# A hybrid decoder layer in float32: the head by token tile, another order of units and transfers, small products in fewer slots

## The chip, the core and the metric

The kernel runs on one core of a Trainium2 chip. The core has TensorE (PE; its weight loads are shown apart as PEld), VectorE (DVE), ScalarE (ACT) and GpSimd (POOL), each with an instruction stream of its own that it works off in order, and SyncE (SP), which here only issues DMA transfers. The engines wait for one another through semaphores. The metric is the device time of one execution in microseconds (us), lower is better. The kernel before takes 151.75 us, the median of 3 runs (151.47 to 152.13).

## What is computed

256 tokens of width 1024 go through a layer norm, one input projection, four causal mixers side by side, an output projection and a last layer norm. Cut to what matters:

```python
h    = layernorm(x, emb_ln_g, emb_ln_b)                 # x: 256 x 1024, float32
proj = h @ w_in                                         # 15 column groups of 256 (and 4 columns for dt)
y_ssd  = ssd(z, conv4(xbc), dt)                         # Mamba-2: causal convolution, silu, chunks of 128
y_hgrn = rms(chunk_scan(q, f = sigmoid(h_f), i)) * silu(h_g)
y_ret  = groupnorm(retention(q, k, v)) * silu(r_g)
y_moba = softmax(q k^T + alibi) v * silu(m_g)           # block-sparse attention, here one own block
y   = concat(y_ssd, y_hgrn, y_ret, y_moba) @ w_out      # 1024 x 1024
out = layernorm(2 ** 0.25 * h + y, ln_g, ln_b)          # 256 x 1024
```

## The kernel before, in words

**Products.** The two projections are done with exact halves of float32: an operand is cast to fp32r (`hi`), and the rest is `lo = x - hi`. A product is then hi·hi + hi·lo + lo·hi. A unit is one column group of 256. It has two halves (128 channels each, or 128 tokens each), and a half is 8 k tiles x 3 products = 24 matmuls of 256 columns, called a slot. There are 15 units, so 30 slots; the output projection follows as slots 30 and up. The order of the units stands in `UNITS`: h_f, h_q, h_i, m_q, m_k, xs, bc, z, m_v, r_q, ... (the prefixes h, m, r are HGRN2, MoBA and retention; xs, bc and z belong to the SSD mixer).

**Weights.** `load_w` issues the DMA of half a unit (512 KB) on SP six slots ahead; `split_hi` casts it to `whi` on ACT four slots ahead, `split_lo` subtracts on DVE to get `wlo`. `begin(slot)` issues these and then the small steps that the table `steps` lists for the slot, and `project(slot)` issues the 24 matmuls. So the table, written by hand, sets where the mixers' work stands in each engine's stream.

**The head.** x comes in four transfers (`xt0`, `xt1`: two token tiles of 128, in halves of 512 columns). DVE takes statistics, POOL raises the variance to -1/2 (`lrs`), DVE and ACT write the normed `xn`, PE transposes it in 16 pieces against a unit matrix `ident` (a part of `ck`, loaded by DMA), ACT applies gain and bias per channel from PSUM (`h_in`: tile `hf`, 128 channels x all 256 tokens), DVE casts to `hhi` and subtracts to `hlo`. Three products of a cleared tile (`warm`) run on PE while x comes in. `first_unit` interleaves the transposes of later k tiles with products of unit h_f; h_q's products fill in until `wlo` of h_f is there. The gains and biases lie in `ch`, loaded by SP's eighth transfer.

**The middle.** The names that matter later: `conv` is the causal convolution (one ACT step into `cacc`, then three DVE steps); `conv_silu` and `z_in` apply SiLU on ACT (`xc`, `zs`), after an ACT_TABLE_LOAD; `ssd_scores` are PE products of `xc` into `scg`; `widen(m)` and `level(m)` are HGRN2's levels (DVE factors `A`, `kk`, then PE products into `lv`); `moba_max` and `moba_exp` are the softmax of a query tile, `moba_scale` multiplies it by the reciprocal sum `msum` on DVE; `ssd_step_a` and `ssd_step_b` compute dt by a softplus in some 20 small DVE steps and then let POOL build `ra` by `affine_select`.

Of the kernel before, what the change touches and what calls it, by code (L numbers as in the profile page):

```python
# [119 lines left out]
def hybrid_layer(  # L120
# [114 lines left out]
    load_w(0, 1, 2)
    nc.sync.dma_start(ck[:, P:], consts[:, P:])
    for j in range(2):
        load_w(1, j)
# [2 lines left out]
    rw = cp.tile([P, R_SMALL], F32, name="rw")
    nc.sync.dma_start(rw, rows[:, 0:R_SMALL].to_broadcast([P, R_SMALL]))
    for j in range(2):
        load_w(2, j)
# [50 lines left out]
    trb = {}  # L295

    def h_transpose(k, T):
        if T == 0:
            trb[k] = bank(f"tr{k}")
        nc.tensor.transpose(trb[k][:, T * P:(T + 1) * P], xn[T][:, k * P:(k + 1) * P], ident)  # L300

    hfs = {}

    def h_in(k):
        hf = hfs[k] = sb([P, SEQ], f"hf{k}", tag="hf", bufs=4)
        g, b = ch[:, C_EG + k:C_EG + k + 1], ch[:, C_EB + k:C_EB + k + 1]
        if k == 0:
            nc.scalar.activation(hhi[:, k, :], trb[k][:, :SEQ], AF.Identity, scale=g, bias=b)
            nc.vector.tensor_scalar(hf, trb[k][:, :SEQ], g, b, op0=ALU.mult, op1=ALU.add)
            return  # L310
        nc.scalar.activation(hf, trb[k][:, :SEQ], AF.Identity, scale=g, bias=b)
        if k == KT - 1:
            nc.scalar.copy(hhi[:, k, :], hf)
        else:
            nc.vector.tensor_copy(hhi[:, k, :], hf)
        h_rest(k - 1)
        if k == KT - 1:
            h_rest(k)

    def h_rest(k):  # L320
        nc.vector.tensor_sub(hlo[:, k, :], hfs[k], hhi[:, k, :].bitcast(F32))

    for k in range(4):
        h_transpose(k, 0)
    for k in range(4):
        h_transpose(k, 1)
    for k in range(4):
        h_in(k)
    split_hi(0, 1, 2, (0,))

# [1 line left out]
    ps_of, hq = {}, {}  # L332

    def first_unit():
        """Both halves of unit 0 side by side, as the k tiles come in."""
        ps = [bank(f"pj_h_f{n}")[:, :SEQ] for n in range(2)]
        ps_of["h_f", 0], ps_of["h_f", 1] = ps

        def part(k, q):
            l = (whi, whi, wlo)[q][0, k // 4][:, k % 4]  # L340
            r = (hhi, hlo, hhi)[q]
            for n in range(2):
                nc.tensor.matmul(ps[n], l[:, n * P:(n + 1) * P], r[:, k, :], start=(k == 0 and q == 0),  # L343
                                 stop=(k == KT - 1 and q == 2))
        for k in range(KT):
            if k < 4:
                h_transpose(k + 4, 0)
                h_transpose(k + 4, 1)
                h_in(k + 4)
            if k == 1:  # L350
                split_hi(0, 1, 2, (1,), nc.vector.tensor_copy)
            part(k, 0)
            if k:
                part(k - 1, 1)
        part(KT - 1, 1)
        split_lo(0, 0, 2, (1,))
        split_lo(0, 1, 2)
        split_hi(1, 0)
        split_hi(1, 1)
        project(2, (0, 1))  # L360
        for k in range(KT):
            part(k, 2)
        project(3, (0, 1))
# [755 lines left out]
```

## Time and profile before

| | before |
|---|---|
| median of 3 runs | 151.75 us (151.47 to 152.13) |
| span of the profiled execution | 150.6 us |
| PE busy | 138.5 us, 92% |
| PEld busy | 127.7 us, 85% |
| DVE busy | 116.5 us, 77% |
| ACT busy | 74.8 us, 50% |
| POOL busy | 17.8 us, 12% |
| the chain that ended last, by engine | PE 56%, DVE 20%, ACT 8%, DMA 6% |

The span reaches from the first to the last recorded instruction of the profiled execution, and is all that is known of that execution's own time; the median of the timed runs is 1.15 us above it. In the profile a row names the engine, the line of the kernel, the operation, what it writes and reads, and its duration; in brackets stands how long the engine was idle just before and which instruction released it. Matmuls are pipelined: what one costs is read from start to start, not from its duration.

### The profile page before, as it was taken

The numbers are of one execution on the slowest core, as the hardware profiler recorded it, in microseconds if no ns is written. First come the engines' busy times: TensorE is split into PE (matmuls) and PEld (weight loads), VectorE is DVE, ScalarE is ACT, GpSimd is POOL, SyncE is SP. The second block draws the span as 40 slices with busy tenths as digits, with TensorE's granted clock in tenths as the row PEclk, the third lists the DMA queues.
The fourth block names the chain that finished last, engine by engine and source line by source line (L and its number), as shares of the span: only waits on it lengthen the run. The fifth ranks groups of instructions, "written<-read, shape, count | busy, mean of one in ns | idle before, by whom it ended". The sixth has DMA issues, their size and how long they took to land.

```text
span 150.6 us, 3259 instructions
## 1 busy us (share of the span) xinstructions
PE 138.5 (92%) x1320; PEld 127.7 (85%) x1320; DVE 116.5 (77%) x240; ACT 74.8 (50%) x120; POOL 17.8 (12%) x23
## 2 busy tenths in 40 slices
PE   6859999999999999999999999998999999999900
PEld 3149999999999998999999999997999988888800
DVE  2589968988596397969899999859379899168681
ACT  3079978552451759699919722062663764000000
POOL 4230000000000000000062063050004000004040
PEclk9986999999999999999999999999999999999995
DMA  4998299998748431656517800689804450000304
GB/s 151 275 406 324 69 325 325 307 327 319 197 133 255 138 80 59 168 189 232 190 65 256 308 0 0 159 310 364 270 23 139 140 139 4 0 0 0 139 0 139
DMA packets 9390, 26.07 MB, mean 173 GB/s; under 512 B 1056, under 2 KB 1696, under 8 KB 9120
## 3 DMA queue, kind: packets, MB, share of 16 engines
q1 hardware_dynamic: 9376, 25.87, 52.2%
q8 instruction: 10, 0.16, 0.4%
q14 instruction: 4, 0.03, 0.1%
HBM read 24.82 MB, written 1.05 MB: 172 GB/s over the span
## 4 chain that ended last, share of the span: by engine, by line
PE 56%; DVE 20%; ACT 8%; DMA 6%; issue 3%; POOL 2%; SPq 1%; POOLq 1%; DVEq 0%; ACTq 0%
PE po L979 5%; PE po L980 5%; PE po L978 5%; PE pj_h_f L343 4%; PE pj_m_q L406 4%; PE pj_xs L406 4%; PE pj_m_k L406 4%; PE pj_m_g L406 4%; PE pj_h_q L406 4%; PE pj_h_i L406 4%; PE pj_r_g L406 4%; DMA xt<-in_x_dram 3%; DMA ret<-in_ret_dram 3%; PE pj_bc L406 2%; ACT pe L842 2%
## 5 line engine op out<-in xcount | busy, mean ns | idle before, releaser
L979 PE MATMUL po<-wlo_wo,yhi 128*128 128x512 f32 (+1 forms) x40 | 14.0, 349 | 0.0
L978 PE MATMUL po<-whi_wo,yhi 128*128 128x512 f32 (+1 forms) x40 | 14.0, 349 | 0.0
L980 PE MATMUL po<-whi_wo,ylo 128*128 128x512 f32 (+1 forms) x40 | 13.9, 347 | 0.0
L222 ACT CAST whi_wo<-wr_wo 128x1024 fp32r<-128x1024 f32 x8 | 8.3, 1047 | 5.3 <-PE pj_h_g L406 2.2
L231 DVE TENSOR_TENSOR wlo_wo<-wr_wo,whi_wo 128x1024 fp32r<-128x1024 f32 x8 | 9.6, 1218 | 0.0
L693 POOL TENSOR_SCALAR_AFFINE_SELECT ra<-ahi 128x1024 fp32r<-128x1024 f32 x1 | 1.1, 1101 | 65.6 <-DVE ahi L689 65.6
L978 PEld LDWEIGHTS po<-whi_wo,yhi 128*128 128x128 f32 x40 | 7.5, 188 | 1.0
L980 PEld LDWEIGHTS po<-whi_wo,ylo 128*128 128x128 f32 x40 | 7.5, 188 | 1.0
L979 PEld LDWEIGHTS po<-wlo_wo,yhi 128*128 128x128 f32 x40 | 7.5, 188 | 1.0
L986 DVE TENSOR_TENSOR xn<-xn,po 128x512 f32<-128x512 f32 (+1 forms) x5 | 2.9, 579 | 5.8 <-PE po L980 5.8
L176 PE MATMUL warm<-warm 128*128 128x512 f32 x6 | 5.5, 1082 | 1.5 <-DVE warm L173 1.5
L637 DVE SCALAR_TENSOR_TENSOR cacc_xs<-pj_xs,ch,cacc_xs 128x255 f32<-128x255 f32 (+2 forms) x6 | 2.9, 482 | 4.6 <-ACT cacc_xs L635 4.4
L300 PEld LDWEIGHTS tr<-ck,xn 128*128 128x128 f32 x16 | 2.3, 171 | 4.1 <-DVE xn L276 4.1
L300 PE MATMUL tr<-ck,xn 128*128 128x128 f32 x16 | 3.6, 351 | 2.3 <-DVE xn L276 2.3
L263 DVE BATCH_NORM_STATS2 lst<-xt 128x6 f32<-128x512 f32 x4 | 2.8, 694 | 3.6 <-DMA xt<-in_x_dram 3.6
L842 ACT ACTIVATE pe<-pe,mmax 128x128 f32<-128x128 f32 (+1 forms) x8 | 3.5, 445 | 3.0 <-DVE mmax L835 3.0
L176 PEld LDWEIGHTS warm<-warm 128*128 128x128 f32 x6 | 1.8, 326 | 3.6 <-issue 2.1
L222 ACT CAST whi_h_f<-wr_h_f 128x512 fp32r<-128x512 f32 x3 | 1.9, 617 | 6.1 <-DMA wr_h_f<-in_w_dram 6.1
L406 PE MATMUL pj_h_g<-whi_h_g,hhi 128*128 128x256 f32 x16 | 4.7, 294 | 0.0
L406 PE MATMUL pj_m_q<-hhi,whi_m_q 128*128 128x256 f32 x16 | 4.7, 293 | 0.0
L406 PE MATMUL pj_r_k<-hhi,whi_r_k 128*128 128x256 f32 x16 | 4.7, 293 | 0.0
L406 PE MATMUL pj_m_v<-whi_m_v,hhi 128*128 128x256 f32 x16 | 4.7, 292 | 0.0
(298 smaller groups left out, 544.7 us busy)
## 6 DMA issues: line engine op xcount, KB each, us to landing
wr_wo<-in_wo_dram SPq DMA_DIRECT2D x8, 512.0 KB, 4.0
rb<-in_rows_dram SPq DMA_DIRECT2D x2, 1024.0 KB, 7.7
wr_z<-in_w_dram SPq DMA_DIRECT2D x2, 520.0 KB, 6.3
xt<-in_x_dram SPq DMA_DIRECT2D x4, 256.0 KB, 3.4
wr_h_f<-in_w_dram SPq DMA_DIRECT2D x4, 256.0 KB, 5.2
wr_h_q<-in_w_dram SPq DMA_DIRECT2D x2, 512.0 KB, 5.2
wr_h_i<-in_w_dram SPq DMA_DIRECT2D x2, 512.0 KB, 5.0
wr_m_q<-in_w_dram SPq DMA_DIRECT2D x2, 512.0 KB, 4.9
```

The lines of the kernel that those rows point to most:

```text
L176: nc.tensor.matmul(wb, warm[:, :P], warm, start=True, stop=True)
L222: copy(whi[i, j][:, r, :], t[:, r, :])
L231: nc.vector.tensor_sub(wlo[i, j][:, r, :], t[:, r, :], whi[i, j][:, r, :].bitcast(F32))
L300: nc.tensor.transpose(trb[k][:, T * P:(T + 1) * P], xn[T][:, k * P:(k + 1) * P], ident)
L343: nc.tensor.matmul(ps[n], l[:, n * P:(n + 1) * P], r[:, k, :], start=(k == 0 and q == 0), stop=(k == KT - 1 and q == 2))
L406: nc.tensor.matmul(ps, l, r, start=(n == 0), stop=(n == len(seq) - 1))
L637: nc.vector.scalar_tensor_tensor(a_[:, d:], ps[:, :SEQ - d], tap(3 - d), a_[:, d:], op0=ALU.mult, op1=ALU.add)
L842: nc.scalar.activation(pt[:, h, :], pt[:, h, :], AF.Exp, bias=mmax[:, i:i + 1], accum_out=msum[:, i:i + 1])
L978: nc.tensor.matmul(po[T, c0], yhi[:, k, ts], hi, start=(i == 0 and j == 0), stop=False)
L979: nc.tensor.matmul(po[T, c0], yhi[:, k, ts], lo, start=False, stop=False)
L980: nc.tensor.matmul(po[T, c0], ylo[:, k, ts], hi, start=False, stop=(i == 3 and j == 1))
L986: nc.vector.tensor_add(xn[T][:, cs], xn[T][:, cs], po[T, cs.start])
```

## The change

The unit order becomes h_i, z, h_f, h_q, m_q, m_k, xs, bc, m_v, ... The first two units are taken token-major (tokens as rows of the product), so that a product needs one token tile of `hhi` and `hlo` only. A function `head()` writes out the order of everything up to slot 4, and the slots then start at 4 (h_f).

```diff
+    idt = cp.tile([P, P], F32, name="idt")          # unit matrix, built on POOL; no longer loaded
+    nc.gpsimd.memset(idt, 1.0)
+    nc.gpsimd.affine_select(out=idt, in_=idt, pattern=[[1, P]], compare_op=ALU.is_equal, fill=0.0,
+                            base=0, channel_multiplier=-1)
+    nc.tensor.matmul(wb[:, :P], warm[:, :P], warm[:, :P], start=True, stop=True)
...
-    load_w(0, 0, 2)
+    load_w(0, 0)
     nc.sync.dma_start(ch, chan)
+    for q in (1, 2, 3, 4):
+        load_w(*divmod(q, 2))
...
+    def h_in(T, hf):
+        hfs[T, hf] = sb([P, 4, P], f"hf{T}{hf}", tag=HF_TAG[T, hf])
+        for k in range(4):
+            kk_ = 4 * hf + k
+            nc.scalar.activation(hfs[T, hf][:, k, :], trb[T, hf][:, k, :], AF.Identity,
+                                 scale=ch[:, C_EG + kk_:C_EG + kk_ + 1],
+                                 bias=ch[:, C_EB + kk_:C_EB + kk_ + 1])
...
+    def head():
+        pool = nc.gpsimd.tensor_copy
+        ln_stats(0, 0)
+        ln_stats(0, 1)
+        ln_scale(0)
+        ln_stats(1, 0)
+        for c in range(4):
+            ln_apply(0, c * 256, c * 256 + 256)
+        h_transpose(0, 0)
+        h_transpose(0, 1)
+        split_hi(0, 0, 2, (0,), pool)
+        split_hi(0, 0, 2, (1,), pool)
+        h_in(0, 0)
+        h_hi(0, 0, 0, 2)
+        ln_stats(1, 1)
+        h_hi(0, 0, 2, 4)
+        ln_scale(1)
...
+        split_hi(0, 1)
+        h_in(0, 1)
+        ln_apply(1, 0, 512)
...
+        h_hi(0, 1, 0, 4)
+        h_lo(0, 0)
+        h_lo(0, 1)
+        split_hi(1, 0, 1, None, pool)
+        split_hi(1, 1, 1, None, pool)
+        first("h_i", 0, 0)
+        first("h_i", 0, 1)
+        h_transpose(1, 0)
+        h_transpose(1, 1)
+        h_in(1, 0)
+        h_in(1, 1)
+        first("z", 0, 0)
+        first("z", 0, 1)
+        h_hi(1, 0, 0, 4)
+        h_hi(1, 1, 0, 4)
+        h_lo(1, 0)
+        h_lo(1, 1)
+        for name in ("h_i", "z"):
+            first(name, 1, 0)
+            first(name, 1, 1)
+        split_hi(2, 0)
+        for q in range(4):
+            split_lo(*divmod(q, 2))
+        for name in ("h_i", "z"):
+            for T in range(NT):
+                first(name, T, 2)
...
-            nc.vector.tensor_scalar(pt[:, h, :], pt[:, h, :], msum[:, i:i + 1], None, op0=ALU.mult)
+            nc.scalar.mul(pt[:, h, :], pt[:, h, :], msum[:, i:i + 1])
...
-        16: [level64, lambda: widen(64), lambda: conv_silu("xs", 0), lambda: z_in(0), lambda: z_in(1),
-             lambda: conv_silu("bc", 2), level64_in, lambda: moba_scale(1)],
+        17: [level64, lambda: widen(64), lambda: conv(3, "bc"), level64_in, lambda: moba_scale(1), ssd_ra],
+        18: [level128, lambda: conv_silu("xs", 0), z_silu, lambda: conv_silu("bc", 2), level128_in,
+             lambda: load_rows(0)],
```

`first(name, T, part)` issues 8 matmuls: part 0 is hi·hi, part 1 hi·lo of h, part 2 the `wlo` product. Beside this the softplus moves from slot 17 to slot 5 and POOL's `ra` becomes a step `ssd_ra` of its own in slot 17; `z_in` only copies z, and SiLU of it is the step `z_silu`; three early weight halves go into tiles that are free at that time; groups of small products stand in 15 places between slots instead of 17. The numbers of matmuls in the projections do not change.

On ACT the first rows are, before (rows of the instruction stream, with the semaphores they wait for; a DMAHW semaphore is a transfer's, 7 is `ch` here):

```order
L222 ACT_TABLE_LOAD
L222 CAST whi_h_f_130<-wr_h_f_90 128x512 [waits DMAHW5_49]
L273 ACTIVATE xn_110<-xt_69,lnb,lrs_115 128x512 [waits DMAHW1_49,DVE_49]
L222 CAST whi_h_f_130<-wr_h_f_90 128x512 [waits DMAHW6_49]
L308 ACTIVATE hhi<-tr_141,ch 128x256 [waits DMAHW7_49,PE_49]
L311 ACTIVATE hf_156<-tr_143,ch 128x256 [waits PE_49]
L311 ACTIVATE hf_160<-tr_145,ch 128x256 [waits PE_49]
```

and in the changed kernel, where semaphore 5 is that of `ch`:

```order
L296 ACT_TABLE_LOAD [waits DMAHW5_49]
L296 ACTIVATE hf_196<-tr_183,ch 128x128 [waits PE_49]
L296 ACTIVATE hf_196<-tr_183,ch 128x128 x3
L229 CAST whi_h_i_208<-wr_h_i_96 128x1024 [waits DMAHW6_49]
L296 ACTIVATE hf_210<-tr_188,ch 128x128 [waits PE_49]
L296 ACTIVATE hf_210<-tr_188,ch 128x128 x3
L346 ACTIVATE xn_116<-xt_70,lnb,lrs_121 128x512 [waits DMAHW3_49,DVE_49]
```

The table load stood without a wait; now it stands behind the wait for `ch`, and the cast of a weight half stands between the two halves of `h_in` of tile 0.

On DVE the changed head reads (tile 0's `hhi` and `hlo` are written from hf_196 and hf_210, lmv_118 and xn_116 are of tile 1):

```order
L301 CAST hhi<-hf_196 128x2x128 [waits Activation_49]
L272 BN_AGGR lmv_118<-lst_123 128x2 [waits DVE_49]
L273 TENSOR_SCALAR lrs_121<-lmv_118 128x1 [waits DVE_49]
L342 SCALAR_TENSOR_TENSOR lnb<-lmv_118,lrs_121 128x1 [waits Pool_49]
L277 TENSOR_SCALAR xn_116<-xt_70,lmv_118,lrs_121 128x512
L301 CAST hhi<-hf_210 128x4x128 [waits Activation_49]
L306 TENSOR_TENSOR hlo<-hf_196,hhi 128x4x128
L306 TENSOR_TENSOR hlo<-hf_210,hhi 128x4x128 [waits DVE_49]
```

Tile 0's `hlo` stands behind the norm of tile 1. Before, each k tile's `hlo` stood right behind its cast.

In the middle, ACT's stream between the softmax of MoBA's second query tile and the SiLU that `ssd_scores` reads was:

```order
L842 ACTIVATE pe,msum<-pe,mmax 128x256
L635 ACTIVATE cacc_bc<-pj_bc,ch 128x256
L222 CAST whi_r_k_972<-wr_r_k_850 128x1024 [waits DMAHW0_49,PE_49]
L641 ACT_TABLE_LOAD
L641 ACTIVATE xc<-cacc_xs 128x512
L648 ACTIVATE zs<-pj_z_891 128x256
L648 ACTIVATE zs<-pj_z_945 128x256 [waits PE_49]
L641 ACTIVATE xc<-cacc_bc 128x512 [waits DVE_49,Activation_49]
```

and is now:

```order
L858 ACTIVATE pe,msum<-pe,mmax 128x256
L643 ACTIVATE cacc_bc<-pj_bc,ch 128x256 [waits PE_49]
L229 CAST whi_r_k_1027<-wr_r_k_906 128x1024 [waits DMAHW6_49]
L643 ACTIVATE cacc_bc<-pj_bc,ch 128x256 [waits DVE_49]
L580 COPY yh<-lv_1029 64x4x64 [waits PE_49]
L580 COPY yh<-lv_1030 64x4x64 [waits PE_49]
L875 ACTIVATE pe<-pe,msum 128x256 [waits DVE_49,Activation_49]
L875 ACTIVATE pe<-pe,msum 128x256 [waits Activation_49] x3
L229 CAST whi_r_v_1082<-wr_r_v_975 128x1024 [waits DMAHW7_49,PE_49]
L649 ACT_TABLE_LOAD
L649 ACTIVATE xc<-cacc_xs 128x512
L660 ACTIVATE zs<-zs 128x512
```

One more step of the convolution, two copies, four scalings and one more cast have come between.

## Rows read from the trace of the kernel before

**Rows 1.** The page: busy time of each engine; one group of DVE.
```profile
PE 138.5 (92%) x1320; PEld 127.7 (85%) x1320; DVE 116.5 (77%) x240; ACT 74.8 (50%) x120; POOL 17.8 (12%) x23
...
L231 DVE TENSOR_TENSOR wlo_wo<-wr_wo,whi_wo 128x1024 fp32r<-128x1024 f32 x8 | 9.6, 1218 | 0.0
```

**Rows 2.** Timeline, PE, head: start us, us, what, count [idle before <- releaser].
```profile
8.96 0.66 PE L300 MATMUL tr<-ck,xn 128*128 128x128 f32 x4 [1.98 <-DVE xn L276]
...
22.38 2.03 PE L406 MATMUL pj_h_q<-hhi,wlo_h_q 128*128 128x256 f32 x16
24.24 0.28 PE L406 MATMUL pj_h_i<-whi_h_i,hhi 128*128 128x256 f32 x1
```

**Rows 3.** Timeline, DVE, head.
```profile
7.26 0.69 DVE L263 BATCH_NORM_STATS2 lst<-xt 128x6 f32<-128x512 f32 x1 [1.16 <-DMA xt<-in_x_dram]
...
10.27 0.68 DVE L231 TENSOR_TENSOR wlo_h_f<-wr_h_f,whi_h_f 128x512 fp32r<-128x512 f32 x1
...
14.34 0.42 DVE L222 CAST whi_h_f<-wr_h_f 128x512 fp32r<-128x512 f32 x1
```

**Rows 4.** Windows: busy us (count) by engine, granted PE clock, DMA share, GB/s.
```profile
10.50:13.50 3.00, 3.00 (x16) 2.92 (x15) 2.82 (x10) 3.00 (x7) 0.31 (x1) 0.50 0.99 367
```

**Rows 5.** Timeline, ACT, head.
```profile
0.78 1.28 ACT L222 ACT_TABLE_LOAD   x1 [0.78 <-PEq L1106]
...
10.79 1.47 ACT L311 ACTIVATE hf<-tr,ch 128x256 f32<-128x256 f32 x3
```

**Rows 6.** Timeline, SP: the issue of ch.
```profile
4.06 0.43 SPq L234 DMA_DIRECT2D ch<-in_chan_dram  x1
```

**Rows 7.** DMA issues: count, KB each, median us to landing.
```profile
ch<-in_chan_dram SPq DMA_DIRECT2D x1, 19.0 KB, 5.0
```

**Rows 8.** Timeline, ACT: two forms with 128 columns.
```profile
55.55 0.39 ACT L842 ACTIVATE pe<-pe,mmax 128x128 f32<-128x128 f32 x1
...
79.26 0.60 ACT L736 COPY scx<-scg 128x128 f32<-128x128 f32 x2 [3.38 <-DVE sm L734]
```

**Rows 9.** Timeline, POOL: its only cast.
```profile
10.79 0.31 POOL L656 CAST upr<-ck 128x128 fp32r<-128x128 f32 x1 [1.48 <-DMA ck<-in_consts_dram]
```

**Rows 10.** Timeline, POOL, 74 to 82 us.
```profile
76.72 1.10 POOL L693 TENSOR_SCALAR_AFFINE_SELECT ra<-ahi 128x1024 fp32r<-128x1024 f32 x1 [65.61 <-DVE ahi L689]
77.77 2.07 POOL L693 TENSOR_SCALAR_AFFINE_SELECT ra<-alo 128x1024 fp32r<-128x1024 f32 x1
```

**Rows 11.** Timeline, DVE, 74 to 80 us.
```profile
76.76 2.13 DVE L231 TENSOR_TENSOR wlo_r_k<-wr_r_k,whi_r_k 128x1024 fp32r<-128x1024 f32 x1
```

**Rows 12.** Timeline, ACT, 62 to 71 us.
```profile
63.42 0.51 ACT L842 ACTIVATE pe<-pe,mmax 128x256 f32<-128x256 f32 x1 [1.43 <-DVE mmax L835]
...
65.52 0.56 ACT L635 ACTIVATE cacc_bc<-pj_bc,ch 128x256 f32<-128x256 f32 x1
65.98 1.04 ACT L222 CAST whi_r_k<-wr_r_k 128x1024 fp32r<-128x1024 f32 x1
67.04 1.28 ACT L641 ACT_TABLE_LOAD   x1
68.33 0.64 ACT L641 ACTIVATE xc<-cacc_xs 128x512 f32<-128x512 f32 x1
...
69.40 0.63 ACT L641 ACTIVATE xc<-cacc_bc 128x512 f32<-128x512 f32 x1
69.92 0.75 ACT L573 COPY yh<-lv 64x256 f32<-64x256 f32 x2
```

**Rows 13.** Timeline, PE, 60 to 80 us.
```profile
64.99 0.28 PE L406 MATMUL pj_z<-wlo_z,hhi 128*128 128x260 f32 x1
65.20 0.68 PE L568 MATMUL lv<-A,kk 64*64 64x64 f32 x16
...
72.65 0.84 PE L729 MATMUL scg<-xc 64*128 64x128 f32 x12
```

**Rows 14.** Timeline, DVE, 60 to 68 us.
```profile
66.12 1.52 DVE L637 SCALAR_TENSOR_TENSOR cacc_bc<-pj_bc,ch,cacc_bc 128x255 f32<-128x255 f32 x3 [1.11 <-ACT cacc_bc L635]
```

More of the change, by code (lines that the diff above doesn't have):

```diff
@@ L231, in split_lo @@
             nc.vector.tensor_sub(wlo[i, j][:, r, :], t[:, r, :], whi[i, j][:, r, :].bitcast(F32))
-    load_w(0, 0, 2)
+    load_w(0, 0)
     nc.sync.dma_start(ch, chan)
[L235 to L238, printed above, removed]
+    for q in (1, 2, 3, 4):
+        load_w(*divmod(q, 2))
+    rw = cp.tile([P, R_SMALL], F32, name="rw")
+    nc.sync.dma_start(rw, rows[:, 0:R_SMALL].to_broadcast([P, R_SMALL]))
+    for q in (5, 6, 7):
+        load_w(*divmod(q, 2))
+    nc.sync.dma_start(ck, consts)
     lev = cp.tile([P, 5, 64], I32, name="lev")
     nc.sync.dma_start(lev, lev_tab)
[L241 to L244, printed above, removed]
     def row(n):
@@ L293, in hybrid_layer @@
     hhi = cp.tile([P, KT, SEQ], F32R, name="hhi")
     hlo = cp.tile([P, KT, SEQ], F32R, name="hlo")
[L295 to L344, printed above, removed]
-        for k in range(KT):
[L346 to L363, printed above, removed]
@@ new lines, in h_hi, with h_lo, first @@
+    def h_hi(T, hf, k0, k1):
+        nc.vector.tensor_copy(hhi[:, 4 * hf + k0:4 * hf + k1, T * P:(T + 1) * P],
+                              hfs[T, hf][:, k0:k1, :])
+    def h_lo(T, hf):
+        ks, ts = slice(4 * hf, 4 * hf + 4), slice(T * P, (T + 1) * P)
+        nc.vector.tensor_sub(hlo[:, ks, ts], hfs[T, hf], hhi[:, ks, ts].bitcast(F32))
+    ps_of = {}
+    def first(name, T, part):
+        i = names.index(name)
+        if part == 0:
+            ps_of[name, T] = bank(f"pj_{name}{T}")
+        ps = ps_of[name, T][:, :UCOLS[name]]
+        l = (hhi, hlo, hhi)[part]
+        r = (whi, whi, wlo)[part]
+        for k in range(KT):
+            nc.tensor.matmul(ps, l[:, k, T * P:(T + 1) * P], r[i, k // 4][:, k % 4],
+                             start=(part == 0 and k == 0), stop=(part == 2 and k == KT - 1))
@@ L367, in project @@
+    def project(slot):
         i, j = divmod(slot, 2)
@@ L399, in trip @@
                 return (hhi[:, k, ts], hi), (hlo[:, k, ts], hi), (hhi[:, k, ts], lo)
-        seq = [(k, q) for k in range(KT) for q in range(3)]
-        if slot < 4:
-            seq.sort(key=lambda kq: kq[1] == 2)
-        for n, (k, q) in enumerate(seq):
-            if q in parts:
+        for k in range(KT):
+            for q in range(3):
                 l, r = trip(k)[q]
-                nc.tensor.matmul(ps, l, r, start=(n == 0), stop=(n == len(seq) - 1))
+                nc.tensor.matmul(ps, l, r, start=(k == 0 and q == 0), stop=(k == KT - 1 and q == 2))
     yhi = cp.tile([P, KT, SEQ], F32R, name="yhi")
@@ L614, in h_values @@
     def h_values():
-        nc.scalar.copy(hv, ps_of["h_i"])
+        for T in range(NT):
+            nc.scalar.copy(hv[:, T, :], ps_of["h_i", T][:, :DB])
     def gate(name, tag):
@@ L1052, in begin @@
             st()
-        if slot < 34:
-            split_lo(*divmod(slot + 4, 2))
-    first_unit()
+        for q in LO.get(slot, (slot + 4,) if slot < 34 else ()):
+            split_lo(*divmod(q, 2))
+    head()
     lower_bound()
-    for q in (2, 3):
-        split_lo(*divmod(q, 2))
-    for slot in range(s0):
+    for slot in range(4, s0):
         begin(slot)
-        if slot > 1:
-            project(slot, (2,) if slot < 4 else (0, 1, 2))
+        project(slot)
     order = [(i, T, n) for i, T in ((0, 0), (1, 0), (2, 0), (0, 1), (3, 0))
```

142 lines of the change are left out of this document (69 added, 73 removed).

## The prediction

> **What bounds the kernel now.** I read the page's busy times first: TensorE is busy 92% of the span [rows 1], so time is lost or won where TensorE waits, and elsewhere only where another engine's work comes too late for it. Then the timeline of PE: it waits in the head, until the first transposes at 8.96, and later only by tenths. From there a unit of work is a matmul of 256 columns, 0.117 us from start to start: the 16 products of wlo_h_q begin at 22.38, the next product at 24.24, (24.24 - 22.38) / 16 [rows 2]. The third unit, the first one that both kernels treat alike in full, begins at 24.24. I use that moment as the head's clock: what it moves by, the end moves by, as long as TensorE stays full behind it. The timelines of DVE, ACT, POOL and SP over the first 16 us show the head's chain; those from 60 to 80 us show the stretch in which the SSD scores are prepared.
>
> The sums are made against the profiled execution, span 150.6; the median of the runs is 151.75, so I add differences to the median.
>
> **The head.** Before, the statistics of tile 1's second half (7.26 to 7.95) stood ahead of tile 0's norm on DVE [rows 3], and this goes: the changed kernel can transpose tile 0 about 1.5 us earlier, from some 7 to 8.3. What is late next is ACT's `h_in`.
> - *Its start.* The changed stream has the table load behind the wait for `ch`. Before, that load ran at 0.78 beside the transfers of x [rows 5]. `ch` was issued at 4.06 [rows 6] and landed 5.0 us later [rows 7], at 9.07. Ahead of it in the queue one issue and 64 KB less now stand, so I take 8.6 (8.0 to 9.1). The load takes 1.28 [rows 5], so `h_in` starts at 9.9.
> - *Its length.* 16 steps of 128 columns replace 8 of 256 (0.49 each, 1.47 for three [rows 5]). The same form with 128 columns isn't there; a plain copy of 128 columns takes 0.60 for two, about 0.27 from start to start, and an exponential of 128 columns, also with a per-partition bias, takes 0.39 [rows 8]. I take the latter: half tile (0,0) is ready at 9.9 + 4 x 0.39 = 11.5, then the cast of a weight half, 1.04 [rows 12], ends at 12.5, half tile (0,1) at 14.1.
> - *Tile 0's hlo.* DVE casts 512 columns in 0.42 and subtracts 512 in 0.68 [rows 3]: the first hlo would stand at 15.2.
> - *POOL beside DVE.* In the trace a `wlo` that takes 1.22 elsewhere [rows 1] took 2.13 at 76.76 [rows 11], when POOL had begun an affine_select of 1.10 at 76.72; POOL's next one, queued, took 2.07 [rows 10]. 76.72 + 1.10 and then some 1.05 is just the end of the `wlo`: one stood still while the other ran. In the changed head POOL casts two halves of z (128x1040) just when DVE writes xn, hhi and hlo; both sets are released by the same power step of tile 1, near 12.9. POOL's only cast, 128x128, took 0.31 [rows 9], which scaled up by 8 is 2.5; the select of 1024 columns took 1.10 and is the nearer row by size. I take 1.1. The delay to hlo is then between nothing (POOL waits) and 1.8 (two casts, less the gap), or more with casts of 2.5. I take 0.8: first hlo at 16.0.
> - *From there to the third unit.* 8 products (hi·lo of tile 0, the second four wait for the next hlo at 16.6) to 17.1; 8 transposes, 0.107 each (four within 0.66, of which the last one's latency isn't paid), to 18.0; then `h_in` of tile 1, 8 x 0.39 from 17.5 to 20.6, its casts and hlo to 22.2 on DVE. TensorE has z's 16 products of tile 0 to 19.9, waits about 0.9 in all in h_i's 16 of tile 1, ends these at 22.7, z's 16 at 24.6, and the 32 `wlo` products at 28.3. The four `wlo` (1.22 each) are done in the same stretch, from 22.2 to 26.9, ahead of the products that read them. Third unit at 28.4 instead of 24.24: **+4.2**.
> - *Bounds.* With the load ahead of `ch`, steps of 0.27 and no collision the first hlo stands at 12.8, and the third unit begins at 24.0: -0.2. With POOL casts of 2.5 and the low clock at hand (0.50 granted from 10.5 to 13.5 [rows 4], when TensorE had been idle for 1.98; the level is 1.2 instead of 2.4 GHz) for the tile-0 products after their second wait, it is 31: +6.6.
>
> The Trainium skill has a rule for the collision ("SBUF — State Buffer", section on the engine ports): DVE and GpSimd share one pair of SBUF ports, it is an exclusive lock held for a whole instruction, and DVE takes it when it has two SBUF inputs or a doubled mode. The rows above agree, to 0.1 us. By the rule hlo (two SBUF inputs), xn and hhi are all exposed, and the delay would be the 1.8 end, a third unit at 29.4; without it 27.6. It speaks against moving the casts of the first two units to POOL.
>
> **The middle.** Before, `scg` began at 72.65 [rows 13]; its input xc was ready at 69.40 + 0.63 = 70.03 [rows 12], so the chain had 2.6 to spare. That chain began with the softmax of MoBA's second tile at 63.42, in slot 15, and `scg` stood in slot 18. Now they are in slots 16 and 19: again three slots, so TensorE arrives 72.65 - 63.42 = 9.2 after the first exponential. On ACT there lie between, now: four exponentials to 65.52, 2.1; a convolution step, 65.98 - 65.52 = 0.46; a cast, 1.04; a second convolution step, 0.46; two copies, 0.65; four scalings; a cast, 1.04; the table load, 1.28; three SiLU of 512 columns, (70.03 - 68.33) = 1.7 with z in the same number of columns [rows 12]. A scaling of 256 columns on ACT isn't in the trace; an exponential of 256 takes 0.5 a step, and I take that: 2.0. Sum 10.7, late by 1.5. But the scalings also wait for the reciprocal on DVE, which now stands behind three convolution steps of 1.52 together [rows 14], a `wlo` of 1.22, widen(64) (about 0.8: two subtract-like operations of 256 columns, half of 0.68 each, and a small one), and three more steps, 1.52: 5.1 after the first convolution step of ACT ends at 2.6, and with the reciprocal 7.8 after the first exponential. Then 2.0 + 1.04 + 1.28 + 1.7 = 6.0: xc at 13.8, late by 4.6. Nothing on TensorE covers it, since it works in order and `scg` stands ahead of half of r_q; level128, which reads widen(64), waits for a part of the same time. **+4.6**, bounds 0 (if the softmax begins 5 earlier relative to the slots) and 5.5.
>
> **The rest.** Two groups of small products fewer. A change costs about 0.1 in and 0.1 out: the last z product starts at 64.99, `lv` at 65.20, 0.21 instead of 0.117 [rows 13]. **-0.4**. The 8 scalings leave DVE and the softplus moves to slot 5: DVE isn't the bound while TensorE waits, so 0. One warm product more and the unit matrix from POOL: before x is there, 0. The tail from the output projection on is the same: 0.
>
> Sum: 151.75 + 4.2 + 4.6 - 0.4 = 160.15, forecast **160.2 us**.
>
> **Rivals.**
> - *Only the head is late* (0.20). The softmax is ready early, since DVE has fewer operations in the middle, and xc comes in time: 151.75 + 4.2 - 0.4 = 155.5. For it: DVE had idle time there, 1.11 ahead of the convolution's steps [rows 14], and loses 8 operations. Against: the ACT chain alone is 1.5 too long.
> - *Only the middle is late* (0.10). The head breaks even: 151.75 + 4.6 - 0.4 = 156.0.
> - *Faster* (0.14). Tile 0's chain on ACT is short enough. Its place is the first hlo: from there 8 products, 8 transposes and 80 products are 0.94 + 0.86 + 9.4 = 11.2, so if it is ready before 12.7 the third unit begins ahead of 23.9 and, with -0.4 and no wait at `scg`, the kernel is ahead by over 0.7. With the load ahead of `ch`, steps of 0.27 and transfers 0.8 earlier it is 12.0: third unit at 23.2, 151.75 - 1.0 - 0.4 = 150.3. For it: transposes are possible 1.5 earlier. Against: the order has the load behind the wait.
> - *No change* (0.05): the head even, the chain in time, 151.4.
> - *A table load costs twice what its row shows* (0.02), since ACT stands still behind it once more: the load behind `ch` and the one ahead of SiLU are both on the path, 160.2 + 2 x 1.28 = 162.8. Against: the load at 67.04 took 1.28, and the next ACTIVATE began at 68.33 [rows 12], at once. The Trainium skill states this cost ("ScalarE: Activation LUTs", section "What ACT_TABLE_LOAD costs"): 1283 ns and then a drain of some 1380 ns for each change of set; the trace agrees with the first part and does not show the second.
>
> **How the numbers follow.** The forecast, both late, has 0.49; its own range is 156.5 to 163.5 (head +2.5 to +6.6, middle +2.5 to +5.5). The likeliest time is 160.2. The range for 8 in 10 must take in the two half cases and most of the head's bounds: 151.0 to 164.0, which leaves out the faster case and a little above. A measurement of this kernel can tell about 0.5%, 0.76 us, from no change. Faster by more than that 0.14, within it 0.05, slower 0.49 + 0.20 + 0.10 + 0.02 = 0.81.
>
> **What would show it.** In the profile after: an ACT_TABLE_LOAD that starts where `ch` lands, not at 0.8; the first `h_in` near 10; h_i's first products of tile 0, then a gap on PE of 3 us or more before the hi·lo products at 16; z casts on POOL beside stretched xn, hhi or hlo on DVE; the first h_f product at 28.4 (27 to 30). In the middle: `scg` released by ACT's SiLU after a wait of PE of some 4 us (with level128's), ACT idle before L875 with DVE's reciprocal as the releaser. I am wrong in the head if the first h_f product comes before 25, and in the middle if PE waits under 1 us ahead of `scg`.

## The result, and the profile after

The changed kernel takes 164.57 us, the median of 4 runs (164.07 to 166.06), against 151.61 beside it: 1.0852 times the time before (95% interval 1.0795 to 1.0909), 13.0 us slower. The forecast was 160.2 with a range to 164.0: the direction and the places were right, the size was too small. The profiled execution has a span of 162.7 (its own time 164.45), 12.1 more than before. The other 0.9 is for the most part no cost of the change: in every run of both kernels whose span is known the time lies 1.7 to 1.8 above the span, so the profiled execution of the kernel before, with its span of 150.6, took some 152.3, which is 0.6 to 0.7 above that kernel's medians. All rows of before come from it. One execution in all, the longest of experiment c (166.71), lies over 1.5% above the shortest of its kernel, and c's ratio leaves it out.

The page of the changed kernel: busy times, and two of the rows of 40 slices (tenths; PEclk is the granted clock).

```profile
PE 143.3 (88%) x1322; PEld 131.3 (81%) x1322; DVE 116.4 (72%) x226; ACT 77.7 (48%) x133; POOL 19.9 (12%) x28
...
PE   6933999999999999998919999999989999999910
...
PEclk9975599999999999999996999999999999999996
```

TensorE is busy longer than before [rows 1] with one product more, and there are two dents in both rows: slices 3 to 5 and around 21. These are the head and the wait ahead of `scg`.

**The head.** The timeline of ACT, then of DVE and POOL (start us, us, what, count, [idle before <- releaser]):

```profile
8.13 1.28 ACT L296 ACT_TABLE_LOAD   x1 [8.13 <-DMA ch<-in_chan_dram]
9.42 1.51 ACT L296 ACTIVATE hf<-tr,ch 128x128 f32<-128x128 f32 x4
10.81 1.06 ACT L229 CAST whi_h_i<-wr_h_i 128x1024 fp32r<-128x1024 f32 x1
11.75 1.53 ACT L296 ACTIVATE hf<-tr,ch 128x128 f32<-128x128 f32 x4
...
18.79 2.90 ACT L296 ACTIVATE hf<-tr,ch 128x128 f32<-128x128 f32 x8 [4.62 <-PE tr L289]
```

```profile
12.33 0.98 DVE L342 SCALAR_TENSOR_TENSOR lnb<-lmv,lrs 128x1 f32<-128x1 f32 x1 [0.67 <-POOL lrs L274]
13.24 1.34 DVE L277 TENSOR_SCALAR xn<-xt,lmv,lrs 128x512 f32<-128x512 f32 x1
...
14.83 1.28 DVE L306 TENSOR_TENSOR hlo<-hf,hhi 128x512 fp32r<-128x512 f32 x2
```

```profile
12.25 2.05 POOL L229 CAST whi_z<-wr_z 128x1040 fp32r<-128x1040 f32 x2
```

The load does stand behind `ch` (before, it ran at 0.78 [rows 5]); a step of `h_in` takes 0.35 from start to start; POOL's casts of z, 1.02 each, begin at 12.25, and the one-column lnb beside them takes 0.98 (0.16 in experiment d, without these casts). The first hlo is done near 15.5. Then TensorE, and its granted clock by stretches (us, busy of PE, PEld, DVE, ACT, POOL, clock, DMA share, GB/s):

```profile
10.70 1.56 PE L320 MATMUL pj_h_i<-whi_h_i,hhi 128*128 128x256 f32 x4 [2.48 <-DVE hhi L301]
14.96 1.23 PE L320 MATMUL pj_h_i<-whi_h_i,hhi 128*128 128x256 f32 x4 [2.69 <-DVE hhi L301]
15.99 1.91 PE L320 MATMUL pj_h_i<-whi_h_i,hlo 128*128 128x256 f32 x8
17.69 1.91 PE L289 MATMUL tr<-idt,xn 128*128 128x128 f32 x8
19.25 1.60 PE L320 MATMUL pj_z<-whi_z,hhi 128*128 128x260 f32 x8
...
29.70 0.28 PE L413 MATMUL pj_h_f<-hhi,whi_h_f 128*128 128x256 f32 x1
```

```profile
8.50:10.00 1.50, 0.00 (x0) 0.00 (x0) 0.00 (x0) 1.49 (x3) 0.60 (x2) 0.96 1.02 407
10.00:12.00 2.00, 1.26 (x4) 1.00 (x4) 1.36 (x5) 2.00 (x5) 0.26 (x1) 0.50 1.01 414
...
18.00:20.00 2.00, 2.00 (x11) 2.00 (x10) 0.00 (x0) 1.21 (x4) 0.29 (x1) 0.50 0.20 74
20.00:22.00 2.00, 2.00 (x18) 2.00 (x17) 0.70 (x2) 2.00 (x6) 0.00 (x0) 0.97 0.00 0
```

TensorE stood still twice for over 2 us, and the clock is at 0.50 (1.2 of 2.4 GHz) from 9.9 to 20.1, where before it was low from 10.25 to 13.67 [rows 4 lie in it]. From 14.96 a product takes 0.21 from start to start, and a transpose about as much. The first h_f product comes at 29.70, 5.46 later than the third unit's first before [rows 2].

**The middle.** ACT from the softmax of MoBA's second tile to the SiLU; TensorE; POOL and DVE ahead of `lv`; and TensorE's clock behind `scg`:

```profile
71.80 0.51 ACT L858 ACTIVATE pe<-pe,mmax 128x256 f32<-128x256 f32 x1
...
76.51 0.75 ACT L580 COPY yh<-lv 64x256 f32<-64x256 f32 x2
79.42 1.71 ACT L875 ACTIVATE pe<-pe,msum 128x256 f32<-128x256 f32 x4 [2.16 <-DVE msum L871]
81.03 1.03 ACT L229 CAST whi_r_v<-wr_r_v 128x1024 fp32r<-128x1024 f32 x1
82.08 1.28 ACT L649 ACT_TABLE_LOAD   x1
...
84.43 0.61 ACT L649 ACTIVATE xc<-cacc_bc 128x512 f32<-128x512 f32 x1
```

```profile
74.03 0.77 PE L575 MATMUL lv<-A,kk 64*64 64x64 f32 x16 [0.92 <-DVE F L521]
...
85.09 1.65 PE L745 MATMUL scg<-xc 64*128 64x128 f32 x12 [3.39 <-ACT xc L649]
86.67 1.11 PE L764 MATMUL xst<-idt,xc 128*128 128x128 f32 x4
87.58 1.00 PE L864 MATMUL mpt<-idt,pe 128*128 128x128 f32 x4
```

```profile
72.18 1.09 POOL L709 TENSOR_SCALAR_AFFINE_SELECT ra<-alo 128x1024 fp32r<-128x1024 f32 x1 [33.76 <-DVE mmax L847]
72.22 1.32 DVE L517 TENSOR_TENSOR A<-A,F 128x256 f32<-128x256 f32 x1
```

```profile
85.00:86.00 1.00, 0.91 (x8) 0.91 (x10) 0.00 (x0) 0.98 (x4) 0.00 (x0) 0.50 0.00 0
...
88.00:89.00 1.00, 1.00 (x9) 1.00 (x8) 1.00 (x2) 0.38 (x1) 0.00 (x0) 0.80 0.00 0
89.00:90.00 1.00, 1.00 (x11) 1.00 (x10) 0.86 (x2) 0.66 (x4) 0.00 (x0) 1.00 0.00 0
```

ACT waits 2.16 for the reciprocal, xc is ready at 85.04, 13.2 after the first exponential (before: 6.6 [rows 12]), and TensorE waits 3.39 for it. Then the clock is low once more, from 85.0 to 88.4, and the 12 `scg` products take 1.58 from start to start instead of 0.77 before [rows 13].

**The ledger.** I split each execution at the first product of the third unit. Before: 24.24, and 118.2 from there to TensorE's last product. After: 29.70 and 125.1. Of the 6.9 in the second part 3.39 are the wait at `scg`, 0.92 that at `lv`, and 1.5 the low clock behind `scg`: scg, xst and mpt take 4.12 from start to start, and 2.63 in the same order at the full clock (experiment a; 2.33 before). Some 1.1 is left, of which 0.56 lies in the y transposes; I did not follow it further.

### The profile page after: what moved, and what is told of

Read it like the earlier page. It is cut to its first block, busy times and chain, and to the rows that moved or that the text cites. A ratio compares the mean times of both kernels' runs of the same rounds, so it can differ in the third digit from the quotient of the medians.

```text
span 162.7 us, 3252 instructions
## 1 busy us (share of the span) xinstructions
PE 143.3 (88%) x1322; PEld 131.3 (81%) x1322; DVE 116.4 (72%) x226; ACT 77.7 (48%) x133; POOL 19.9 (12%) x28
## 4 chain that ended last, share of the span: by engine, by line
PE 62%; DVE 14%; ACT 9%; DMA 5%; issue 3%; POOL 2%; SPq 1%; POOLq 1%; DVEq 0%; ACTq 0%
PE po L994 5%; PE po L995 5%; PE po L996 5%; PE pj_h_i L320 4%; PE pj_z L320 4%; PE pj_xs L413 4%; PE pj_m_k L413 4%; PE pj_m_g L413 4%; PE pj_h_f L413 3%; PE pj_r_g L413 3%; PE pj_m_q L413 3%; PE pj_h_q L413 3%; DMA ch<-in_chan_dram 3%; DMA ret<-in_ret_dram 2%; PE pj_r_k L413 2%
## 5 line engine op out<-in xcount | busy, mean ns | idle before, releaser
L320 PE MATMUL pj_h_i<-whi_h_i,hhi 128*128 128x256 f32 x16 | 4.0, 381 | 5.2 <-DVE hhi L301 5.2
L296 ACT ACTIVATE hf<-tr,ch 128x128 f32<-128x128 f32 x16 | 5.9, 469 | 4.6 <-PE tr L289 4.6
L320 PEld LDWEIGHTS pj_h_i<-whi_h_i,hhi 128*128 128x128 f32 x16 | 3.0, 252 | 6.1 <-issue 3.0
L301 DVE CAST hhi<-hf 128x512 fp32r<-128x512 f32 (+1 forms) x5 | 1.8, 367 | 7.7 <-ACT hf L296 7.7
L517 DVE TENSOR_TENSOR A<-A,F 128x256 f32<-128x256 f32 x6 | 3.4, 574 | 3.1 <-PE lv L538 3.1
L709 POOL TENSOR_SCALAR_AFFINE_SELECT ra<-alo 128x1024 fp32r<-128x1024 f32 x1 | 1.1, 1092 | 33.8 <-DVE mmax L847 33.8
L911 DVE TENSOR_TENSOR rq<-pj_r_q,ret 128x512 f32<-128x512 f32 x1 | 0.7, 692 | 6.0 <-DMA ret<-in_ret_dram 6.0
L258 POOL TENSOR_SCALAR hrs<-hss 128x8 f32<-128x8 f32 x1 | 1.1, 1100 | 29.8 <-DVE hss L611 29.8
L413 PE MATMUL pj_r_q<-hhi,whi_r_q 128*128 128x256 f32 x16 | 4.7, 295 | 0.0
L413 PE MATMUL pj_xs<-hhi,whi_xs 128*128 128x256 f32 x16 | 4.7, 294 | 0.0
```

Of the source, the lines that this page charges most:

```text
L296: nc.scalar.activation(hfs[T, hf][:, k, :], trb[T, hf][:, k, :], AF.Identity, scale=ch[:, C_EG + kk_:C_EG + kk_ + 1], bias=ch[:, C_EB + kk ...
L301: nc.vector.tensor_copy(hhi[:, 4 * hf + k0:4 * hf + k1, T * P:(T + 1) * P], hfs[T, hf][:, k0:k1, :])
L320: nc.tensor.matmul(ps, l[:, k, T * P:(T + 1) * P], r[i, k // 4][:, k % 4], start=(part == 0 and k == 0), stop=(part == 2 and k == KT - 1))
L413: nc.tensor.matmul(ps, l, r, start=(k == 0 and q == 0), stop=(k == KT - 1 and q == 2))
L517: nc.vector.tensor_mul(Av[:, :, 1, :], Av[:, :, 1, :], Fv[:, :, 0:1].to_broadcast([P, nb, m]))
```

## The experiments

The kernels e, g, h, i, j and k build on a, f and l on the kernel before; the ratios are to the kernel before, run beside them. It took 151.54 beside a to d, 152.24 beside e to h, and 151.83 beside i to l, so between these groups the ratios compare better than the medians. The edits are cut to the changed lines and what shows their place; "..." marks a cut, and a letter the run where several share a listing.

**a_scale_late: the four scalings out of SiLU's way.**
```diff
-    17: [..., level64_in, lambda: moba_scale(1), ssd_ra],
-    18: [level128, ..., lambda: conv_silu("bc", 2), level128_in, ...],
+    17: [..., level64_in, ssd_ra],
+    18: [level128, ..., lambda: conv_silu("bc", 2), lambda: moba_scale(1), level128_in, ...],
```


> Changed kernel, with moba_scale(1) taken out of slot 17 and put behind conv_silu(bc) in slot 18; nothing else. Theory (the wait of 3.4 us ahead of scg comes from the four scalings on ACT, which stand in front of SiLU's table load and wait there for DVE's reciprocal): xc is ready near 81.3 instead of 85.04, TensorE arrives at 81.7, so the wait goes (under 0.3), and with it the low clock behind it (0.50 from 85.0 to 88.6, worth 1.8): 164.6 - 3.4 - 1.8 = 159.4. Rival (the convolution and the casts alone are too long for two slots): a wait of 1.5 or more is left, and 161.5 to 163.

Measured 159.70, ratio 1.0513 (1.0434 to 1.0592), 4.9 less than the changed kernel. Its ACT:

```profile
78.76 1.28 ACT L649 ACT_TABLE_LOAD   x1
...
81.12 0.62 ACT L649 ACTIVATE xc<-cacc_bc 128x512 f32<-128x512 f32 x1
81.64 1.69 ACT L875 ACTIVATE pe<-pe,msum 128x256 f32<-128x256 f32 x4
```

and its TensorE:

```profile
82.16 0.94 PE L745 MATMUL scg<-xc 64*128 64x128 f32 x12
83.03 0.66 PE L764 MATMUL xst<-idt,xc 128*128 128x128 f32 x4
```

No idle time stands ahead of `scg` any more, and its products run at the full clock. The part behind the third unit's first product is 120.0 instead of 125.1: 5.1, the wait of 3.39, 1.5 of the clock, and 0.2 in small differences. So this order on ACT cost 5 of the 13 us, and some 30% of that was the clock after the wait. The theory held.

**b, c, d: one edit each in the head of the changed kernel.** b: a one-column ACTIVATE ahead of the wait for `ch`. c: 5 and 6 products of the cleared tile in the two gaps. d: z's casts on ACT.
```diff
+    nc.scalar.activation(tl, mhalf[:, :1], AF.Identity)                 # b
+            if (name, T, part) == ("h_i", 0, 0) and k in (0, 4):        # c
+                fill(5 if k == 0 else 6)
-        split_hi(1, 0, 1, None, pool)                                   # d, and (1, 1)
+        split_hi(1, 0)
```


> Changed kernel, with one ACTIVATE (Identity of one column) put on ACT ahead of the wait for ch, so that the first table load runs while x comes in. Theory (h_in waits for the load, 1.28 behind ch): the load stands at about 0.9, the first h_in at 8.1 instead of 9.42, and the first h_f product about 1.0 to 1.6 earlier than 29.70: 163.0 to 163.6. Rival (tile 1's norm and POOL's casts hold back hlo, or the landing of the second weight half): the first h_in is earlier, the first h_f product less than 0.5 earlier, 164.2 to 164.6.

> Changed kernel, with 11 more products of the cleared tile (128 columns, 0.43 us each at the full clock): 5 ahead of h_i's first product of tile 0, 6 between its fourth and fifth. They add no work that anything waits for. Theory (the low clock from about 10 to 20 us is the part of the head's loss that the forecast left out): the granted clock stays 1.00, the tile-0 products and transposes take 0.117 and 0.107 from start to start, and the first h_f product comes at 27.5 to 28.4 instead of 29.70: 162.6 to 163.4. Rival (the low clock is covered by waits for hlo and h_in of tile 1): first h_f product within 0.5 of 29.7, 164.2 to 164.7.

> Changed kernel, with the two casts of z's weight halves on ACT, behind xn of tile 1, instead of on POOL. Theory (POOL and DVE stand still for one another): lnb takes 0.15 instead of 0.98 and xn 0.54 instead of 1.34, the first hlo is done about 1.1 earlier than 15.5, and the first h_f product 0.8 to 1.3 earlier than 29.70: 163.3 to 163.8. Rival (lnb and xn were long for another reason): durations as before, 164.3 to 164.8.

Measured 164.30, 165.01 and 165.38, ratios 1.0836 (1.0754 to 1.0919), 1.0840 (1.0760 to 1.0920) and 1.0876 (1.0789 to 1.0962): none tells from 1.0852, and their intervals are too wide for the effects expected. The profiles show two things that vary between executions. `ch` landed at 8.05 in the changed kernel's profiled execution, and at 9.67, 9.34 and 9.04 in these; a head that waits for this transfer carries its spread of more than 1 us into the time. And the low clock behind `scg`, 3.4 long in the changed kernel's, lasted 6.8 in all three, so that the part behind the third unit's first product took 126.4, 126.0 and 126.3 instead of 125.1. One stretch of it, in b:

```profile
88.00:90.00 2.00, 2.00 (x11) 2.00 (x10) 2.00 (x3) 0.92 (x3) 0.00 (x0) 0.50 0.00 0
```

By the timed runs I count the three as inconclusive; each question is put again below. The traces say more when the head is counted from the landing of `ch`: the first h_f product comes 21.65 behind it in the changed kernel, 20.35 in b, 21.64 in c and 20.47 in d. In a, whose head is that of the changed kernel, it is 21.24, so the same head varies by 0.4. By these single executions the early load is worth 0.9 to 1.3 and z's casts on ACT 0.8 to 1.2, about what was expected. In d, lnb and xn are short, as the theory had it:

```profile
13.31 0.16 DVE L342 SCALAR_TENSOR_TENSOR lnb<-lmv,lrs 128x1 f32<-128x1 f32 x1 [0.67 <-POOL lrs L274]
13.39 0.54 DVE L277 TENSOR_SCALAR xn<-xt,lmv,lrs 128x512 f32<-128x512 f32 x1
```

The profiled execution of c is the one of 166.71, and is read for its clock only: the products ahead of h_i's first took 0.26, not 0.43, left a gap of 2.67, and the clock went to 0.50 all the same, at 13.4.

**e_filled: the gaps filled.**
```diff
+            if (name, T, part) == ("h_i", 0, 0) and k in (0, 4):
+                fill(12 if k == 0 else 12)
```


> a_scale_late (159.7), with 24 more products of the cleared tile on TensorE, 12 ahead of h_i's first product of tile 0 and 12 between its fourth and fifth; with 11, in c_pe_filled, gaps of over 2 us were left and the low clock came all the same (such a product took 0.26, not the 0.43 that was reckoned). Theory (TensorE's standing still brings the low clock, and that is worth 1.5 to 2 in the head): granted clock 1.00 from 8 to 20, tile-0's second products and the transposes at 0.117 and 0.107 a step, first h_f product 1.5 to 2 earlier against the landing of ch, 157.7 to 158.4. Rival (the low clock is covered by other waits of the head): 159.3 to 160.0.

Measured 158.56, ratio 1.0422 (1.0376 to 1.0468), 1.1 less than a by the medians and 1.4 by the ratios. The clock, and the first h_f product at 28.91 with `ch` landed at 8.68 (in a 30.33 with 9.09):

```profile
14.00:16.00 2.00, 1.69 (x15) 1.50 (x14) 2.00 (x3) 0.79 (x1) 0.92 (x1) 1.00 0.99 397
18.00:20.00 2.00, 2.00 (x19) 2.00 (x18) 0.46 (x1) 2.00 (x6) 0.30 (x1) 1.00 0.18 62
```

The clock stays at 1.00, where in a it was 0.50 from 12.0 to 18.8, so it is TensorE's standing still that brings the low one. Counted from the landing of `ch`, the first h_f product comes 1.0 earlier than in a. That is less than the 1.5 to 2 expected. TensorE waits 0.61 for hhi of tile 1 here, but 0.64 in a as well, so this wait doesn't explain the difference, and I did not follow it further.

**g_ch_first: ch ahead of the weights, and the early load.**
```diff
+    nc.sync.dma_start(ch, chan)
     load_w(0, 0)
-    nc.sync.dma_start(ch, chan)
...
+    nc.scalar.activation(tl, mhalf[:, :1], AF.Identity)
```


> a_scale_late (159.7), with ch's transfer issued ahead of the first weight half, and the first table load made early by an ACTIVATE of one column. Theory (h_in, not the landing of x, holds tile 0): the first h_in stands at 7.9 to 8.4, right behind the transposes, instead of 10.5 in that kernel's profile, but the next half tile waits on ACT behind the cast of the second weight half, whose transfer lands near 10.2: h_in of (0,1) ends near 12.7 instead of 14, first h_f product 1.0 to 1.5 earlier, 158.2 to 158.8. Rival (the head hangs on tile 1, not on tile 0's start): 159.4 to 160.0.

Measured 158.19, ratio 1.0390 (1.0364 to 1.0417), 1.5 less than a by the medians and 1.9 by the ratios, and the spread of its runs is 0.6 (1.1 in a). `h_in` begins at 7.69; the first h_f product comes at 28.77 instead of 30.33. As expected.

**k_z_cast_act: the same, with z's casts on ACT.** The edit is that of d.

> g_ch_first (158.19), with the casts of z's weight halves on ACT instead of POOL. In g_ch_first POOL's second cast of z ran at 13.07, and the two hlo of tile 0 beside it took 2.14 instead of 1.29. Theory (they stand still for one another): hlo 1.29, TensorE's hi·lo products and the first h_f product 0.8 earlier, 157.2 to 157.6. Rival (the casts on ACT hold up h_in of tile 1, or hlo isn't what TensorE waits for): 158.0 or more.

Measured 157.62, ratio 1.0376 (1.0345 to 1.0407), 0.2 less by the ratio and 0.6 by the medians. The two hlo on DVE, in g and then in k, and between them POOL in g:

```profile
13.29 2.14 DVE L309 TENSOR_TENSOR hlo<-hf,hhi 128x512 fp32r<-128x512 f32 x2
```
```profile
13.07 1.21 POOL L232 CAST whi_z<-wr_z 128x1040 fp32r<-128x1040 f32 x1 [0.24 <-DMA wr_z<-in_w_dram]
```
```profile
12.94 1.28 DVE L309 TENSOR_TENSOR hlo<-hf,hhi 128x512 fp32r<-128x512 f32 x2
```

The collision is shown (2.14 against 1.28 with nothing else on POOL); the first h_f product comes at 27.55 instead of 28.77. Not all of this 1.2 is the collision: the cast of h_i's second weight half, which waits for its transfer, began 0.35 earlier in k, and the low clock lasted 3.4 instead of 6.8. What the edit is worth in the timed runs lies between nothing and 0.8, since the intervals overlap.

**h_head_reordered: all of tile 0 first.** g, and both `h_in` of tile 0 ahead of the weight cast, hlo of tile 0 ahead of xn of tile 1, tile 1's statistics earlier, z's casts on ACT.
```diff
         h_in(0, 0)
+        ln_stats(1, 1)
+        ln_scale(1)
         h_hi(0, 0, 0, 2)
-        ln_stats(1, 1)
         h_hi(0, 0, 2, 4)
-        ln_scale(1)
+        h_in(0, 1)
+        h_hi(0, 1, 0, 4)
+        split_hi(0, 1)
+        h_lo(0, 0)
+        h_lo(0, 1)
...
-        split_hi(0, 1)
-        h_in(0, 1)
         ln_apply(1, 0, 512)
...
-        h_hi(0, 1, 0, 4)
-        h_lo(0, 0)
-        h_lo(0, 1)
-        split_hi(1, 0, 1, None, pool)
...
+        split_hi(1, 0)
```


> g_ch_first, and besides: both halves of h_in of tile 0 ahead of the cast of the second weight half, tile 1's statistics ahead of tile 0's hhi on DVE, tile 0's hlo ahead of xn of tile 1, z's casts on ACT. Theory (the order on ACT and DVE is what made hlo late): hlo of tile 0 is done near 12 instead of 15.5, first h_f product near 25 to 26.5, 154.3 to 156. Rival (token-major itself costs it, with 16 steps of h_in and tile 1 behind tile 0): first h_f product 28 or later, 157.5 to 159.

Measured 155.84, ratio 1.0232 (1.0197 to 1.0267), 2.3 less than g. The first h_f product comes at 26.63, and tile 0's two hlo begin at 11.29 instead of 13.29. As expected: the order on ACT and DVE made hlo late. The 2.3 hold z's casts too, whose own part k puts between nothing and 0.8.

**i_head_reord_filled: h with the gaps filled.**
```diff
+                fill(4 if k == 0 else 5)
```


> h_head_reordered (155.84), with 9 products of the cleared tile (0.26 each) in TensorE's two gaps in h_i's first products, 4 ahead of the first and 5 ahead of the fifth. Theory (the granted clock of 0.50 from about 11.5 to 18 in that kernel comes from these gaps): 1.00 throughout, first h_f product near 25 instead of 26.6, 154.0 to 154.6. Rival (waits for h_in of tile 1 then take its place): 155.3 or more.

Measured 155.56, ratio 1.0239 (1.0204 to 1.0273): no gain over h. The clock is 1.00 throughout the head, but on ACT `h_in` of tile 1 stands right behind z's casts, with no idle time between (0.32 in h), and TensorE waits for that (ACT, then PE):

```profile
13.38 2.00 ACT L232 CAST whi_z<-wr_z 128x1040 fp32r<-128x1040 f32 x2
15.29 2.89 ACT L299 ACTIVATE hf<-tr,ch 128x128 f32<-128x128 f32 x8
```
```profile
18.68 0.74 PE L329 MATMUL pj_h_i<-whi_h_i,hhi 128*128 128x256 f32 x4 [0.66 <-DVE hhi L304]
```

The rival held: in h the low clock lay beside a wait that takes its place.

**j_ali_own: POOL's second select out of the way.**
```diff
-    ali = sb([P, NH, SEQ], "ali", tag="ra1")
+    ali = sb([P, NH, SEQ], "ali")
```


> i_head_reord_filled, with the ALiBi table in a tile of its own instead of in that of ra1, so that POOL's second affine_select no longer waits for MoBA's last read of it. Theory (that select, 1.1 us on POOL just when DVE widens for level 64, holds DVE, and is TensorE's wait of 0.92 ahead of lv): the select runs with the first one, near 35, the operation on A takes 0.42 instead of 1.32, the wait goes, 0.7 to 0.9 faster than i_head_reord_filled. Rival (level 64 is late since one slot is too short for widen behind the maxima): wait over 0.5 left, no change.

Measured 155.46, ratio 1.0240 (1.0211 to 1.0269): no change from i. The select moved to 34.30, the step on A took 0.42, and the wait of 0.92 at `lv` of level 64 went, but level 128 waits instead:

```profile
74.04 0.72 PE L597 MATMUL lv<-A,kk 64*128 64x128 f32 x8 [1.04 <-DVE kk L527]
```

The mechanism of the theory held and its gain did not: the step on DVE that level 128 waits for begins only 0.3 earlier than in i (kk at 73.47 and 73.77), while TensorE comes 1.2 earlier and so waits there.

**f_before_warm: one more warm product in the kernel before.**
```diff
-WARM = 3
+WARM = 4
```


> The kernel before, with 4 products of the cleared tile instead of 3; nothing else. Theory (TensorE's standing still from 6.98 to 8.96 brought the low clock from 10.25 to 13.67): the gap shrinks to under 1, the clock stays at 1.00 or falls later, the third unit's first product comes 0.5 to 1.2 earlier than 24.24, and the time is 150.4 to 151.1. Rival (the first unit's products wait for h_in anyway, or the clock falls all the same): within 0.3 of 151.6.

Measured 151.84 beside 152.24, ratio 0.9975 (0.9957 to 0.9993): 0.4 us faster, of the 0.5 to 1.2 expected. TensorE's gap ahead of the first transposes is 1.51 instead of 1.98 [rows 2], and the clock stays up where it was 0.50 before [rows 4]:

```profile
10.00:12.00 2.00, 1.84 (x12) 1.57 (x13) 2.00 (x8) 2.00 (x6) 0.29 (x1) 1.00 1.00 402
```

The third unit begins at 23.08 instead of 24.24 [rows 2], more than the time shows; the profiled execution of the kernel before was one of its longer ones, as said above.

**l_before_two: f, with moba_tr(0) moved from slot 17 to 18.**
```diff
-    17: [lambda: load_rows(0), ssd_step_a, ssd_step_b, lambda: moba_tr(0)],
+    17: [lambda: load_rows(0), ssd_step_a, ssd_step_b],
```


> f_before_warm (0.9975 of before), with moba_tr(0) in slot 18 instead of alone in slot 17, so that there is one group of small products fewer. Theory (a group costs about 0.1 on entering and 0.1 on leaving): 0.15 to 0.25 faster than f_before_warm, 0.994 to 0.998 of before. Rival (ACT's copy or moba_av then comes late): not faster than f_before_warm.

Measured 151.55 beside 151.83, ratio 0.9985 (0.9968 to 1.0002): no faster than f. One group of small products fewer is not seen in the time. So f is the version that beats both kernels, by 0.25% over the one before; l, which has the same extra product, is 0.15% ahead, with an interval that reaches 1.

## Why the prediction was right or wrong

- **The head, +4.2: measured +5.5.** The step that failed is the low clock, which I put into the upper bound only. The chain up to hlo was right: load behind `ch` (8.13 for 8.6), `h_in` at 9.4 for 9.9, a step 0.35 for 0.39, first hlo 15.5 for 16.0. That it came so near is in part luck: `h_in` of tile 0 was done 0.8 earlier than reckoned, and the collision cost 0.4 more. From there to the third unit I reckoned 12.4 at the full clock, and it took 14.2: from 14.96 to 20.1 TensorE ran at half the clock. e shows that the clock follows TensorE's standing still, and that filling the gaps gives 1.1 to 1.4 back.
- **The parts of the head.** g shows the load and `ch` (1.5 to 1.9), h the order on ACT and DVE with the casts (2.3). With all of it mended (i) the third unit begins at 26.2, still 1.9 later than before. 0.84 of it are waits for hhi of tile 1, whose `h_in`, 2.9 on ACT, stands behind tile 0's; that part was in my working as a wait of 0.9. The rest is not split. Behind the third unit i still takes 1.6 more than the kernel before.
- **POOL beside DVE.** I took 0.8 of delay and casts of 1.1; the casts took 1.02, lnb was longer by 0.83 and xn by 0.80 than alone. In the trace hlo was delayed by about 1.2, since `h_in` of (0,1) was done at 13.3; in d, without the casts, hlo begins 5.6 behind the landing of `ch` instead of 6.8, and g beside k shows the same collision on hlo. The exclusive lock that the Trainium skill describes ("SBUF — State Buffer", section "SBUF: two separate sides") agrees with all three cases, also for an operation of one column.
- **The middle, +4.6: waits 4.3, and 1.5 more.** The chain was right to some tenths: xc 13.2 after the first exponential (13.8 reckoned), TensorE there after 9.9 (9.2), wait 3.39, and 0.92 at level 64. That second wait I had at level 128 (0.14 there), and its cause, POOL's select beside DVE's step on A, was not in the working. What failed is that a wait was priced at its own length: TensorE came out of it at half the clock. a shows it: the time fell by 4.9 for a wait of 3.39.
- **-0.4 for two groups fewer** is not seen: what the groups cost on entering and leaving beyond 0.117 a product, without the waits, adds up to 2.9 in both kernels (17 and 15 groups), and l shows nothing for one.
- **Rivals.** Both half cases, the faster case and that of no change fell. The table load again cost what its row shows: 82.08 + 1.28, and SiLU at 83.37, so no drain behind it.
- **The range** reached to 164.0 and the time was 164.57; even both upper bounds together, 163.5, lie below it, since the middle's bound had no clock in it. Of the 4.4 that the forecast was short of, the head is 1.3 and the part behind it 2.7: 1.5 of clock, the 0.4 that was not seen and 1.1 not followed, less 0.3 since the waits were shorter than reckoned. The part behind TensorE's last product is 0.2 shorter. Some 0.6 is an error of the base. I added differences from a profiled execution to the median and took the 1.15 between its span and the median for what lies outside the span; by all other runs that is about 1.7, so this execution was a longer one than the median. What the head's clock alone cost is known from e only, 1.1 to 1.4.

## What to carry to other kernels

Price a wait of TensorE at its length plus what the low clock takes from the work behind it: that was 3.4 + 1.5 in the one profiled execution, and about 1 more in three others, where the clock stayed low for longer. Read each engine's stream behind a moved step: what stood ahead of a table load or of a transfer's wait decides more than the engine's busy time. And a gap filled or a collision removed is worth only what the next late operand leaves, as i and j show.

## What the runs showed of the hardware that I had not expected

- The low clock came after a single wait in an otherwise full kernel. In the changed kernel's head it lasted from 9.9 to 20.1, through two bursts of four products with gaps of 2.48 and 2.69 ahead of them; behind the wait of 3.39 at `scg` from 85.0 to 88.4, and behind a wait of the same length 6.8 us in b and d.
- An operation of one column on DVE took 0.98 instead of 0.16 beside a POOL cast of 1.02.
- Transfers in the head land at a time that varies: `ch`, behind 1.5 MB of others, at 8.05, 8.68, 9.04, 9.09, 9.34 and 9.67 in six profiled executions (of the changed kernel, e, d, a, c and b) with the same order on SP.
